# Hybrid S5 / RG-LRU / GLA block on one core: logarithms paced and moved, single PSUM banks in turn, head decays issued later, the FFN turn reordered

## The chip, the cores and the metric

One Trainium2 chip, one NeuronCore. The metric is device microseconds of one execution of the kernel; three runs are at hand.

## The reference, cut to what matters

One layer over 1024 latent tokens and 256 context tokens of width 1024: RMSNorm and modulation give `u` and `uc`; one projection `w_in` feeds three mixers; their outputs are gated, summed, projected and added; then a ConvFFN with a hidden width of 2816 follows. The places that the change touches compute

```python
zl = jnp.split(u @ w_in, cuts, axis=-1)          # ... also uc @ w_in
la = jax.nn.log_sigmoid(zd @ w2[d] + b2[d]) / GLA_TAU        # GLA's log decays, 16 ranks a direction
cum = jnp.cumsum(log_a, axis=3); k_out = k * jnp.exp(cum_last - cum)
y = jax.nn.gelu(y); y * jax.nn.sigmoid(y @ w_glu + b_glu)    # the S5 branch's GLU
hid = dwconv(u @ w_up, conv_w, conv_b, (1, 1))               # FFN, after the second norm
```

## The kernel before, in words

All large matmuls are done in a split form: an operand is held as a rounded high part and a rest, and three matmuls replace one (`mm3`, L283; `lat_steps`, L523; `v_steps`, L710). For a weight tile `split` (L213) makes the high part on ScalarE (`S.copy`, L214) and the rest on the engine named by `lo` (L215), which is GpSimd unless `wblock` (L221) is told otherwise. A weight tile is 128x1024; three buffers hold split tiles, two hold raw ones.

TensorE's order is the order of the text (`pe_order`, L444). The other engines are ordered ahead of time by a scheduler that places each instruction by its estimated time, with the text's order as priority, except in stretches whose order is written out (`norm_order`, L1770, and `turn_order`, L1932). Each engine then runs its list strictly in order. SP's list issues the loads and some stores.

The mixers' serial parts are small, so their TensorE pieces are set between pieces of one long projection stream. `proj_stream` (L743) is a generator; `F(name)` (L867) lets it run for the microseconds of the table `FILL` (L62). The stream's stages end in markers: "ctx", "lru" (context projections; then q, context k and v, and `z_steps`, L680), "pc" (latent k, `v_steps` over the eight latent blocks, "kv"; then g, "g"; the first gated products, "lru branch"; and the rest). `take` (L616) hands out the next split weight tile and `ahead` (L611) starts the following ones, so that up to two wait beyond the one in use.

Beside the stream runs `background` (L671), twelve steps of `decay_logs` (L649): four heads for each of two latent halves (128x512) and for the context (128x256). A step is one small product (two matmul records) into a PSUM bank `sm` (four of these), an Abs and a Relu on ScalarE that free the bank, an Exp, and a polynomial of three rounds, each a Square on ScalarE (L665) and a multiply-add on VectorE (L666) behind a first one (L662). GpSimd subtracts at the end (L667) and SP stores the result. After `z_steps` one step is started per `BG` = 4 us of stream.

In the order of time: the RG-LRU (L935 to L993), S5's prologue (L1014 to L1121, tables of powers, nearly all on VectorE), with `F("s5pro")` of 57.25 us at L1106 and `F("s5pro2")` of 12 us at L1251; eight S5 groups (3 us of stream as `s5st` and two times 1.5 us as `s5tr` in the first) (`s5_matrices`, `s5_states`, `s5_outputs`); the GLU (L1421 to L1460, 22 us of stream ahead of its products); four GLA heads (`Head`, L1278). A head's `decays` (L1284) are two scans (L1287, L1288), a difference (L1299) and an exponential (L1300); `keys` multiplies (L1307); TensorE transposes the result (L1331; `gtr`, 3.37 us of stream, stands ahead of head 0's). `states` ends in a chain of 18 multiply-adds (L1362). Then follow the merge, the output projection (L1709 to L1753, sixteen groups of 24 matmuls, `m` = 0 to 7 in two halves `j`), and the FFN's up-projection as a Strassen-Winograd product of `Pair`s (L1609). Between the two lies the turn (L1770 to L1891), with the second norm of the second half: `sums` and `bcast` on TensorE, `mul`, `sca`, `sub`, `hi`, `lo` on VectorE and ScalarE, and the first products `units(0)` to `units(3)`.

v_steps before takes two weight tiles for each half `hv` and runs two groups of four blocks through both:

```python
ws = take(2)
for b0 in range(0, len(blocks), 4):
    p = two()
    for i, b, k in [(i, b, 4 * kh + k) for kh in range(2) for i, b in enumerate(bs) for k in range(4)]:
```

Of the kernel before, what the change touches and what calls it, by code (L numbers as in the profile page):

```python
# [18 lines left out]
C = 256  # L19
# [18 lines left out]
def _parts(v, bits, n):  # L38
    out = []
    for _ in range(n):  # L40
# [41 lines left out]
        'gbc': [3.31, 3.0, 3.34, 3.52]}  # L82
BG = 4

# [25 lines left out]
def tile_kernel(tc, I, out, dbg=None):  # L110
# [30 lines left out]
    def mm():  # L141
        return psum[1].tile([128, 1024], F32, name=nm("mm"), tag="mm", bufs=psum[2])

    def two():

        return [one(t) for t in "ab"]

    def one(t="a"):
        return psum[1].tile([128, 512], F32, name=nm("m" + t), tag="m" + t, bufs=psum[2])
# [67 lines left out]
    def split_scaled(h, l, src, c):  # L217
        S.activation(h, src, AF.Copy, scale=c)
        V.scalar_tensor_tensor(l, src, c, f32(h), OP.mult, OP.subtract)

# [387 lines left out]

    wsrc, wq = [], [w0]

    def ahead(n):  # L611
        while len(wq) < n and wsrc:
            src = wsrc.pop(0)
            wq.append(wblock(src, src.shape[-1]))

# [33 lines left out]
    def decay_logs(o, n, z, w2):  # L649

        for h in range(4):
            p = sm()
            PE.matmul(p[:, :n], w2[:, h * 128:(h + 1) * 128], z[:, :n], start=True, stop=True)
            par = lsn[0] % 2
            lsn[0] += 1
            e = lsw[0][:, par * 512:par * 512 + n]
            acc = lsw[1][:, par * 512:par * 512 + n]
            S.activation(e, p[:, :n], AF.Abs, bias=vc("b2", h))
            r = tmp()[:, :n]
            S.activation(r, p[:, :n], AF.Relu, bias=nb2[:, h:h + 1], scale=-1.0)  # L660
            S.activation(e, e, AF.Exp, scale=-1.0)
            V.scalar_tensor_tensor(acc, e, LOGQ_R, e, OP.add, OP.mult)  # L662
            for i in range(3):
                q = tmp()[:, :n]
                S.activation(q, e, AF.Square, scale=LOGQ_S, bias=lqb[:, i:i + 1])  # L665
                V.scalar_tensor_tensor(acc, q, LOGQ_C[i], acc, OP.add, OP.mult)  # L666
            G.tensor_tensor(r, r, acc, OP.subtract)  # L667
            SY.dma_start(lsp[h][:, o:o + n], r)
            yield

    def background():  # L671
        zs, w2 = zw[0]
        for j in range(2):
            yield from decay_logs(C + j * 512, 512, zs[j], w2)
        yield from decay_logs(0, 256, zs[2], w2)
        reached.add("ls")

    zw = []

    def z_steps():  # L680
        wz = wraw(I["wz"], 256)
        zh, _ = whl()
        zz = zh[:, 0:512].rearrange("p (k m) -> p k m", k=KT)
        w2 = lsw[3][0:64, 256:768]
        SY.dma_start(w2, I["w2"])
        wz3 = wz.rearrange("p (k m) -> p k m", k=KT)
        S.copy(zz[:, :, 0:32], wz3)
        V.tensor_tensor(zz[:, :, 32:64], wz3, f32(zz[:, :, 0:32]), OP.subtract)
        p = one()
# [4 lines left out]
        zc = lsw[3][0:64, 0:256]  # L694
        S.copy(zc, p[0:64, 0:256])
        p = two()
        for k in range(KT):
            for j in range(2):
                PE.matmul(p[j][0:64], zz[:, k], uh[j][:, k], start=(k == 0), stop=False)
            for j in range(2):  # L700
                PE.matmul(p[j][0:64], zz[:, k], ul[j][:, k], start=False, stop=(k == KT - 1))
            yield 4 * COL
        zs = []
        for j in range(2):
            z = lsw[2][0:64, j * 512:(j + 1) * 512]
            S.copy(z, p[j][0:64])
            zs.append(z)
        zw.append((zs + [zc], w2))

    def v_steps(blocks):  # L710
        for hv in range(2):
            ws = take(2)
            for b0 in range(0, len(blocks), 4):
                bs = blocks[b0:b0 + 4]
                p = two()
                for i, b, k in [(i, b, 4 * kh + k) for kh in range(2) for i, b in enumerate(bs) for k in range(4)]:
                        o = p[i // 2][:, i % 2 * 256:(i % 2 + 1) * 256]
                        h, l = ws[k // 4]
                        sl = slice((k % 4) * 256, (k % 4 + 1) * 256)
                        if b < 2:  # L720
                            ah, al = uch[:, k, b * 128:(b + 1) * 128], ucl[:, k, b * 128:(b + 1) * 128]
                        else:
                            j, bb = divmod(b - 2, 4)
                            ah, al = uh[j][:, k, bb * 128:(bb + 1) * 128], ul[j][:, k, bb * 128:(bb + 1) * 128]
                        last = k == KT - 1 and i % 2 == 1
                        PE.matmul(o, ah, h[:, sl], start=(k == 0 and i % 2 == 0), stop=False, skip_group_check=True)
# [4 lines left out]
                for i0 in range(0, len(bs), 2):  # L731
                    t = pt()
                    S.copy(t, p[i0 // 2])
                    S.dma_start(vsp[bs[i0] * 128:(bs[i0] + 2) * 128, hv * 256:(hv + 1) * 256]
                                .rearrange("(a t) v -> t a v", a=2), t.rearrange("p (a v) -> p a v", a=2))

# [6 lines left out]
    def proj_stream():  # L743
# [12 lines left out]
        yield from both(xl1_out, lru_ctx)  # L756
        yield from marker("lru")
        for b in range(2):
            yield from lat(lambda p: out_rows(p, qsp[b]))
# [251 lines left out]
    def q5(tag=None):  # L1011
        return a5((128, 32), tag)

    lam = a5([128, 96])  # L1014
    SY.dma_start(lam, I["s5lam"])
# [234 lines left out]

    F("s5pro2")  # L1251
    cur = s5_matrices(0)
    for gb in range(8):
# [24 lines left out]
    class Head:  # L1278
# [59 lines left out]
        def states(self):  # L1338
# [22 lines left out]
            for step in range(1, 19):  # L1361
                V.scalar_tensor_tensor(Sd[:, step], Sd[:, step - 1], self.dec[:, step:step + 1], Sd[:, step],  # L1362
                                       OP.mult, OP.add)
            for c0 in (0, 8):
# [68 lines left out]
    for f in range(2):  # L1433
# [9 lines left out]
        V.scalar_tensor_tensor(y, z, 1.0, y, OP.add, OP.mult)  # L1443
        split_scaled(yh5[:, f], yl5[:, f], y, 2.0)
        YG.append(y)
# [20 lines left out]
    head = Head(0)  # L1466
    head.decays()
    head.keys()
# [10 lines left out]
    for h in range(4):  # L1479
# [5 lines left out]
        nxt = Head(h + 1) if h < 3 else None  # L1485
        head.scores(0)
        if nxt:
            nxt.decays()
        F("gsc")
# [119 lines left out]
    class Pair:  # L1609
# [101 lines left out]
    for j in range(2):  # L1711
        sl = tl[j]
        acc = pt()
        for m in range(8):
# [159 lines left out]
    q[0].z6()  # L1874
    q[0].load(3, 4)
    nxt.open("b")
    nxt.p6()
# [10 lines left out]
    q[1].load(3, 4)  # L1888
    q[1].z6()
    q[1].z57()  # L1890
    norm_order.__exit__(None, None, None)  # L1891
# [7 lines left out]
    for i in range(2, HID):  # L1899
# [11 lines left out]
        pair.load(2)  # L1911
        product(pair.D, pair.w[7], T3, True)
        pair.z57()
        pair.load(3, 4)
# [394 lines left out]
```

## Time and profile before

| | us |
|---|---|
| Runs | 1599.44, 1599.78, 1605.92 |
| Median | 1599.78 |
| The profiled execution, its own time | 1601.49 |
| Its span, first to last instruction | 1599.7 |
| TensorE busy in the span | 1521.8 |
| Mean granted TensorE clock | 0.983 of full speed |

The span and the 1.8 us around it make up the profiled execution's own time. Busy shares of a whole span mix stages with different limits, so the rows below are cut by stretches. "PEclk" is the granted share of TensorE's full clock: its two levels are 0.5 (1.2 GHz) and 1.0 (2.4 GHz), so a stretch at 0.95 ran a tenth of its time at the lower one.

### The profile page before, as it was taken

The numbers are of one execution on the slowest core, as the hardware profiler recorded it, in microseconds if no ns is written. First come the engines' busy times: TensorE is split into PE (matmuls) and PEld (weight loads), VectorE is DVE, ScalarE is ACT, GpSimd is POOL, SyncE is SP. The second block draws the span as 40 slices with busy tenths as digits, with TensorE's granted clock in tenths as the row PEclk, the third lists the DMA queues.
The fourth block names the chain that finished last, engine by engine and source line by source line (L and its number), as shares of the span: only waits on it lengthen the run. The fifth ranks groups of instructions, "written<-read, shape, count | busy, mean of one in ns | idle before, by whom it ended". The sixth has DMA issues, their size and how long they took to land. (4 is left out here: it accounts for less than half of the span.)

```text
span 1599.7 us, 21566 instructions
## 1 busy us (share of the span) xinstructions
PE 1521.8 (95%) x8144; PEld 1254.7 (78%) x8144; DVE 1092.8 (68%) x1620; ACT 770.1 (48%) x1221; POOL 461.3 (29%) x291
## 2 busy tenths in 40 slices
PE   5999999799998999999999988999999999999997
PEld 4888867677886788788888767788888888878887
DVE  4533469879876624533461689888888888899962
ACT  4423766665543643443233455444444444444661
POOL 3313333431122323222236534333333333000032
PEclk9999999899999999999999999999999999999999
DMA  9763633221224244231474321222222222974203
GB/s 346 242 224 93 208 109 110 93 90 58 64 61 144 70 139 130 77 86 60 144 246 159 130 88 40 92 80 79 80 91 81 80 80 100 370 248 157 93 27 106
DMA packets 93785, 198.91 MB, mean 124 GB/s; under 512 B 13489, under 2 KB 34865, under 8 KB 93553
## 3 DMA queue, kind: packets, MB, share of 16 engines
q1 hardware_dynamic: 81968, 181.62, 33.9%
q10 hardware_dynamic: 11712, 15.91, 2.9%
q8 instruction: 64, 1.05, 0.3%
q14 instruction: 41, 0.33, 0.1%
HBM read 158.98 MB, written 38.52 MB: 123 GB/s over the span
## 5 line engine op out<-in xcount | busy, mean ns | idle before, releaser
L215 POOL TENSOR_TENSOR wl<-wr,wh 128x1024 fp32r<-128x1024 f32 (+2 forms) x87 | 183.4, 2109 | 455.7 <-ACT wh L214 428.5
L214 ACT CAST wh<-wr 128x1024 fp32r<-128x1024 f32 (+2 forms) x87 | 77.3, 891 | 139.6 <-issue 41.9
L215 POOL TENSOR_TENSOR wp<-tmp,wp 128x512 fp32r<-128x512 f32 x44 | 74.1, 1701 | 220.4 <-ACT wp L214 203.4
L528 PE MATMUL ma<-uh,wh 128*128 128x512 f32 x272 | 118.0, 434 | 4.5 <-ACT pt L795 4.5
L528 PE MATMUL mb<-uh,wh 128*128 128x512 f32 x272 | 107.2, 394 | 0.0
L530 PE MATMUL ma<-ul,wh 128*128 128x512 f32 x272 | 107.0, 393 | 0.0
L530 PE MATMUL mb<-ul,wh 128*128 128x512 f32 x272 | 106.9, 393 | 0.0
L532 PE MATMUL mb<-uh,wl 128*128 128x512 f32 x272 | 106.7, 392 | 0.0
L532 PE MATMUL ma<-uh,wl 128*128 128x512 f32 x272 | 106.4, 391 | 0.0
L214 ACT CAST wp<-tmp 128x512 fp32r<-128x512 f32 x78 | 46.5, 619 | 93.0 <-DVE tmp L1629 92.9
L1693 DVE SCALAR_TENSOR_TENSOR ca<-gv,vec,ca 128x1023 f32<-128x1023 f32 (+2 forms) x66 | 61.4, 954 | 23.7 <-ACT ca L1685 23.6
L214 ACT CAST wp<-hd 128x512 fp32r<-128x512 f32 x88 | 52.8, 618 | 49.1 <-PE bkd L1998 25.9
L214 ACT CAST wp<-wr 128x512 fp32r<-128x512 f32 x97 | 58.2, 620 | 36.4 <-DMA wr<-in_wdn_dram 17.4
L1696 DVE SCALAR_TENSOR_TENSOR ca<-gv,vec,ca 128x1023 f32<-128x1023 f32 (+2 forms) x66 | 70.6, 1093 | 0.1
L528 PEld LDWEIGHTS ma<-uh,wh 128*128 128x128 f32 x272 | 51.8, 190 | 20.7 <-issue 6.5
L2178 POOL TENSOR_TENSOR acc<-acc,tmp 128x256 f32<-128x256 f32 (+1 forms) x9 | 9.0, 1002 | 182.8 <-ACT tmp L2175 182.7
L215 DVE TENSOR_TENSOR wp<-hd,wp 128x512 fp32r<-128x512 f32 x88 | 60.7, 708 | 1.3 <-ACT wp L214 1.1
L530 PEld LDWEIGHTS ma<-ul,wh 128*128 128x128 f32 x272 | 51.6, 190 | 11.5
L532 PEld LDWEIGHTS ma<-uh,wl 128*128 128x128 f32 x272 | 51.4, 189 | 11.5
L532 PEld LDWEIGHTS mb<-uh,wl 128*128 128x128 f32 x272 | 51.3, 189 | 11.4
L530 PEld LDWEIGHTS mb<-ul,wh 128*128 128x128 f32 x272 | 51.3, 189 | 11.3
L528 PEld LDWEIGHTS mb<-uh,wh 128*128 128x128 f32 x272 | 52.0, 191 | 9.5 <-issue 1.4
(628 smaller groups left out, 4661.9 us busy)
## 6 DMA issues: line engine op xcount, KB each, us to landing
wa<-in_ada_dram SPq DMA_DIRECT2D x96, 256.0 KB
wr<-in_wup_dram SPq DMA_DIRECT2D x46, 512.0 KB
wr<-in_win_dram SPq DMA_DIRECT2D x40, 512.0 KB
wr<-in_wdn_dram SPq DMA_DIRECT2D x22, 512.0 KB
hd<-hid SPq DMA_DIRECT2D x22, 512.0 KB
hid<-ca SPq DMA_DIRECT2D x21, 512.0 KB
wr<-in_wout_dram SPq DMA_DIRECT2D x16, 512.0 KB
tmp<-in_wdn_dram SPq DMA_DIRECT2D x22, 256.0 KB
```

Source lines behind the costliest of these rows:

```text
L214: S.copy(h, src)
L215: lo.tensor_tensor(l, src, f32(h), OP.subtract)
L528: PE.matmul(p[j], h[:, kk], uh[j][:, k], start=f, stop=False)
L530: PE.matmul(p[j], h[:, kk], ul[j][:, k], start=False, stop=False)
L532: PE.matmul(p[j], l[:, kk], uh[j][:, k], start=False, stop=e)
L1693: V.scalar_tensor_tensor(a[:, t0_ + 1:t0_ + 1 + n1], x[:, o:o + n1], fw[0], a[:, t0_ + 1:t0_ + 1 + n1], OP.mult, OP.add)
L1696: V.scalar_tensor_tensor(a[:, t0_ + c - 1:t0_ + n - 1], x[:, o + c:o + n], fw[2], a[:, t0_ + c - 1:t0_ + n - 1], OP.mult, OP.add)
L2178: G.tensor_tensor(acc, acc, sq, OP.add)
```

## The change

- `BG` goes from 4 to 6: a step of the logarithms per 6 us of stream. The context's steps come first.
- In `decay_logs` the Relu's output moves from a `tmp` buffer to `lsw[3]`, and the last subtraction goes from GpSimd to VectorE. The second latent half of z lies in partitions 64 to 127, with a second copy of `w2` there (one more load).
- `z_prep` loads and splits the weights of z at the start of the stream's stage after "lru"; they lie in a `tmp` buffer and no longer in a split-weight buffer.
- `one()` takes PSUM banks of the kinds a and b in turn. `v_steps` opens a bank for every two blocks at once, takes one weight tile at a time, runs all blocks through it, and copies each bank out as its last matmul is issued.
- `rests[0]`: between L1014 and L1254 the rests of the stream's weight tiles are made by VectorE.
- Head 0's decays are ordered on VectorE behind the last split of the GLU's input, and the next head's behind the last multiply-add of this head's states (`tc.issue_after` orders the block's instructions on the given instruction's own engine behind it).
- In the output projection four subtractions go from GpSimd at `m` = 1 to VectorE at `m` = 3 (second half). In the turn q[1].p1 stands before `sums`, one product before `bcast`, and z57's copy of bank C is a step of its own, `c57`, set before `hi(5, 2)` and, for q[1], where it was.

The diff, cut:

```diff
-BG = 4
+BG = 6
...
-    def one(t="a"):
+    def one(t=None):
+
+        if t is None:
+            ones_[0] += 1
+            t = "ab"[ones_[0] % 2]
...
-            wq.append(wblock(src, src.shape[-1]))
+            wq.append(wblock(src, src.shape[-1], rests[0]))
...
-            r = tmp()[:, :n]
+            r = lsw[3][:, par * 512:par * 512 + n]
...
-            G.tensor_tensor(r, r, acc, OP.subtract)
+            V.tensor_tensor(r, r, acc, OP.subtract)
...
-        zs, w2 = zw[0]
+        zs, zc, w2 = zw[0]
+        yield from decay_logs(0, 256, zc, w2[0])
         for j in range(2):
-            yield from decay_logs(C + j * 512, 512, zs[j], w2)
-        yield from decay_logs(0, 256, zs[2], w2)
+            yield from decay_logs(C + j * 512, 512, zs[j], w2[j])
...
-    def z_steps():
+    def z_prep():
+
+
         wz = wraw(I["wz"], 256)
-        zh, _ = whl()
-        zz = zh[:, 0:512].rearrange("p (k m) -> p k m", k=KT)
-        w2 = lsw[3][0:64, 256:768]
-        SY.dma_start(w2, I["w2"])
+        zz = tmp([128, 512], F32R).rearrange("p (k m) -> p k m", k=KT)
+        w2 = [lsw[2][64 * j:64 * j + 64, 512:1024] for j in range(2)]
+        for w in w2:
+            SY.dma_start(w, I["w2"])
...
         for hv in range(2):
-            ws = take(2)
-            for b0 in range(0, len(blocks), 4):
...
+            p = [one("ab"[(i + hv) % 2]) for i in range(len(blocks) // 2)]
+            for kh in range(2):
+                (h, l), = take()
+                for i, b in enumerate(blocks):
+                    o = p[i // 2][:, i % 2 * 256:(i % 2 + 1) * 256]
+                    for k in range(4):
...
+                    if kh and i % 2:
+                        t = pt()
+                        S.copy(t, p[i // 2])
...
     def v_steps(blocks):
...
         for hv in range(2):
-            ws = take(2)
-            for b0 in range(0, len(blocks), 4):
...
+            p = [one("ab"[(i + hv) % 2]) for i in range(len(blocks) // 2)]
+            for kh in range(2):
+                (h, l), = take()
+                for i, b in enumerate(blocks):
+                    o = p[i // 2][:, i % 2 * 256:(i % 2 + 1) * 256]
...
+                    if kh and i % 2:
+                        t = pt()
+                        S.copy(t, p[i // 2])
...
         yield from marker("lru")
+        z_prep()
...
+    rests[0] = V
     lam = a5([128, 96])
...
     F("s5pro2")
+    rests[0] = G
...
-        split_scaled(yh5[:, f], yl5[:, f], y, 2.0)
+        glu_last = split_scaled(yh5[:, f], yl5[:, f], y, 2.0)
...
-    head.decays()
+    with tc.issue_after(glu_last.ins):
+        head.decays()
...
         if nxt:
-            nxt.decays()
+            with tc.issue_after(head.last.ins):
+                nxt.decays()
...
+        def c57(self):
+            S.copy(self.gv[1][:, tl[0]], self.C)
+
         def z57(self):
             w, z = self.gv[1][:, tl[0]], self.gv[1][:, tl[1]]
-            S.copy(w, self.C)
...
             if j == 1 and m == 3:
+                for k in range(4, KT):
+                    x = hT[k][:, tl[0]]
+                    V.tensor_tensor(x, x, hT[k - 4][:, tl[0]], OP.subtract)
...
-                    if k > 3:
-                        x = hT[k][:, tl[0]]
-                        G.tensor_tensor(x, x, hT[k - 4][:, tl[0]], OP.subtract)
...
+    q[1].p1()
     q[1].sums((5,))
...
-    q[1].p1()
     rq = rstd_cols(st, 4, small[:, 12:16])
+    product(q[0].A, q[0].w[2], B21, False)
...
     bcast(pr, rq, 4)
+    product(q[1].A, q[1].w[2], B21, False)
     for i in range(2):
-        product(q[i].A, q[i].w[2], B21, False)
...
     q[0].load(3, 4)
+    q[0].c57()
...
     q[1].z6()
+    q[1].c57()
     q[1].z57()
```

## Rows read from the trace of the kernel before

**Rows 1.** The page's part on busy time, TensorE's line

```profile
PE 1521.8 (95%) x8144; PEld 1254.7 (78%) x8144; DVE 1092.8 (68%) x1620; ACT 770.1 (48%) x1221; POOL 461.3 (29%) x291
```

**Rows 2.** Busy time by stretch: stretch, length, engines with instruction counts, PEclk, DMA

```profile
200.00:226.00 26.00, 22.12 (x163) 15.44 (x162) 17.43 (x16) 20.34 (x24) 11.02 (x4) 0.93 0.40 128
255.00:336.00 81.00, 67.19 (x445) 60.22 (x446) 71.20 (x171) 54.58 (x93) 34.17 (x18) 0.92 0.28 94
336.00:402.00 66.00, 61.14 (x311) 50.30 (x310) 56.36 (x111) 39.17 (x67) 12.44 (x8) 0.95 0.23 71
490.00:526.00 36.00, 31.35 (x129) 24.64 (x128) 27.70 (x23) 21.52 (x30) 11.58 (x6) 0.91 0.51 145
640.00:672.00 32.00, 28.24 (x163) 22.76 (x162) 20.45 (x30) 14.46 (x25) 7.67 (x5) 0.95 0.22 80
895.00:985.00 90.00, 77.93 (x321) 60.30 (x321) 76.50 (x92) 47.67 (x78) 44.18 (x27) 0.96 0.24 81
```

**Rows 3.** What TensorE waited for, whole span: us in total, times, longest

```profile
PE ma L726 <- ACT wh L214: 7.6, 1, 7.6
...
PE bkc L839 <- ACT gv L1666: 4.6, 1, 4.6
PE ma L528 <- ACT pt L795: 4.5, 2, 3.8
PE ma L691 <- DVE wh L688: 3.9, 1, 3.9
PE sm L653 <- ACT tmp L660: 3.7, 2, 2.8
...
PE sm L285 <- DVE s L219: 2.9, 1, 2.9
PE sm L286 <- POOL wl L215: 2.5, 1, 2.5
PE ma L727 <- POOL wl L215: 2.4, 1, 2.4
...
PE bkb L279 <- DVE pt L1730: 1.6, 1, 1.6
```

**Rows 4.** GpSimd's groups by shape, 217 to 337 us: busy, mean ns, idle before

```profile
L215 POOL TENSOR_TENSOR wl<-wr,wh 128x1024 fp32r<-128x1024 f32 x9 | 24.5, 2727 | 20.1 <-ACT wh L214 20.1
L667 POOL TENSOR_TENSOR tmp<-tmp,lsw 128x512 f32<-128x512 f32 x8 | 14.3, 1793 | 32.4 <-DVE lsw L666 28.6 <-issue 3.8
```

**Rows 5.** VectorE's costliest group by shape, 217 to 337 us

```profile
L666 DVE SCALAR_TENSOR_TENSOR lsw<-tmp,lsw 128x512 f32<-128x512 f32 x24 | 16.4, 683 | 0.2
```

**Rows 6.** Timeline of one VectorE and one GpSimd instruction: start, us, instruction

```profile
303.80 2.54 DVE L662 SCALAR_TENSOR_TENSOR lsw<-lsw 128x256 f32<-128x256 f32 x1 [1.16 <-POOL tmp L667]
...
303.72 2.34 POOL L215 TENSOR_TENSOR wl<-wr,wh 128x1024 fp32r<-128x1024 f32 x1
```

**Rows 7.** Timeline: the first S5 transposes' last operand, and the transposes

```profile
316.53 0.41 DVE L1162 TENSOR_TENSOR s<-s,s 128x256 f32<-128x256 f32 x1
...
335.29 0.38 PE L1166 MATMUL sm<-con,s 128*128 128x128 f32 x2
```

**Rows 8.** VectorE's timeline around the GLU, and TensorE's at head 0's transposes

```profile
501.63 2.82 DVE L1287 TENSOR_TENSOR_SCAN gl<-gl,gl 64x1280 f32<-64x1280 uint8 x1 [1.51 <-DMA gl<-lsp]
...
521.47 1.49 DVE L1307 TENSOR_TENSOR gl<-gl,gl 128x1280 f32<-128x1280 f32 x1 [0.30 <-ACT gl L1300]
...
524.45 1.25 PE L1331 MATMUL sm<-con,gl 128*128 128x128 f32 x10
```

**Rows 9.** ScalarE's timeline in head 1

```profile
662.97 1.27 ACT L1300 ACTIVATE gl<-gl 128x1280 f32<-128x1280 f32 x1 [4.79 <-DVE gl L1299]
```

**Rows 10.** GpSimd's groups, 895 to 985 us

```profile
L1752 POOL TENSOR_TENSOR h<-h,h 128x512 f32<-128x512 f32 x4 | 6.0, 1509 | 8.5 <-DVE B21l L215 8.5
```

**Rows 11.** Timeline at the end of the turn: VectorE, then TensorE

```profile
975.19 0.67 DVE L1667 TENSOR_TENSOR gv<-gv,bkd 128x512 f32<-128x512 f32 x1
...
979.09 0.39 PE L839 MATMUL bkd<-T4h,wp 128*128 128x512 f32 x1
```

More of the change, by code (lines that the diff above doesn't have):

```diff
@@ L142, in mm @@
         return psum[1].tile([128, 1024], F32, name=nm("mm"), tag="mm", bufs=psum[2])
+    ones_ = [0]
     def two():
         return [one(t) for t in "ab"]
-    def one(t="a"):
+    def one(t=None):
+        if t is None:
+            ones_[0] += 1
+            t = "ab"[ones_[0] % 2]
         return psum[1].tile([128, 512], F32, name=nm("m" + t), tag="m" + t, bufs=psum[2])
@@ L218, in split_scaled @@
         S.activation(h, src, AF.Copy, scale=c)
-        V.scalar_tensor_tensor(l, src, c, f32(h), OP.mult, OP.subtract)
+        return V.scalar_tensor_tensor(l, src, c, f32(h), OP.mult, OP.subtract)
     def wblock(src, cols=1024, lo=G):
@@ L607, in gate_out @@
             S.dma_start(tsp[m][:, j * 512:(j + 1) * 512], t)
-    wsrc, wq = [], [w0]
+    wsrc, wq, rests = [], [w0], [G]
     def ahead(n):
@@ L671, in background @@
     def background():
-        zs, w2 = zw[0]
+        zs, zc, w2 = zw[0]
+        yield from decay_logs(0, 256, zc, w2[0])
         for j in range(2):
-            yield from decay_logs(C + j * 512, 512, zs[j], w2)
-        yield from decay_logs(0, 256, zs[2], w2)
+            yield from decay_logs(C + j * 512, 512, zs[j], w2[j])
         reached.add("ls")
-    zw = []
-    def z_steps():
+    zw, zp = [], []
+    def z_prep():
         wz = wraw(I["wz"], 256)
-        zh, _ = whl()
-        zz = zh[:, 0:512].rearrange("p (k m) -> p k m", k=KT)
-        w2 = lsw[3][0:64, 256:768]
-        SY.dma_start(w2, I["w2"])
+        zz = tmp([128, 512], F32R).rearrange("p (k m) -> p k m", k=KT)
+        w2 = [lsw[2][64 * j:64 * j + 64, 512:1024] for j in range(2)]
+        for w in w2:
+            SY.dma_start(w, I["w2"])
         wz3 = wz.rearrange("p (k m) -> p k m", k=KT)
@@ L688, in z_steps @@
         V.tensor_tensor(zz[:, :, 32:64], wz3, f32(zz[:, :, 0:32]), OP.subtract)
+        zp.append((zz, w2))
+    def z_steps():
+        zz, w2 = zp[0]
         p = one()
@@ L693, in z_steps @@
             yield COL
-        zc = lsw[3][0:64, 0:256]
-        S.copy(zc, p[0:64, 0:256])
+        zct = tmp([64, 256])
+        S.copy(zct, p[0:64, 0:256])
         p = two()
@@ L704, in z_steps @@
         for j in range(2):
-            z = lsw[2][0:64, j * 512:(j + 1) * 512]
+            z = lsw[2][64 * j:64 * j + 64, 0:512]
             S.copy(z, p[j][0:64])
             zs.append(z)
-        zw.append((zs + [zc], w2))
+        zw.append((zs, zct, w2))
     def v_steps(blocks):
         for hv in range(2):
-            ws = take(2)
-            for b0 in range(0, len(blocks), 4):
[L714 to L719, printed above, removed]
+            p = [one("ab"[(i + hv) % 2]) for i in range(len(blocks) // 2)]
[4 more added lines that the diff above has]
+                    for k in range(4):
+                        sl = slice(k * 256, (k + 1) * 256)
+                        ka = 4 * kh + k
                         if b < 2:
-                            ah, al = uch[:, k, b * 128:(b + 1) * 128], ucl[:, k, b * 128:(b + 1) * 128]
+                            ah, al = uch[:, ka, b * 128:(b + 1) * 128], ucl[:, ka, b * 128:(b + 1) * 128]
                         else:
                             j, bb = divmod(b - 2, 4)
-                            ah, al = uh[j][:, k, bb * 128:(bb + 1) * 128], ul[j][:, k, bb * 128:(bb + 1) * 128]
-                        last = k == KT - 1 and i % 2 == 1
-                        PE.matmul(o, ah, h[:, sl], start=(k == 0 and i % 2 == 0), stop=False, skip_group_check=True)
+                            ah, al = uh[j][:, ka, bb * 128:(bb + 1) * 128], ul[j][:, ka, bb * 128:(bb + 1) * 128]
+                        last = ka == KT - 1 and i % 2 == 1
+                        PE.matmul(o, ah, h[:, sl], start=(ka == 0 and i % 2 == 0), stop=False, skip_group_check=True)
                         PE.matmul(o, ah, l[:, sl], start=False, stop=False, skip_group_check=True)
@@ L730, in v_steps @@
                             yield 3 * COL
[L731 to L735, printed above, removed]
+                    if kh and i % 2:
+                        t = pt()
+                        S.copy(t, p[i // 2])
+                        S.dma_start(vsp[(b - 1) * 128:(b + 1) * 128, hv * 256:(hv + 1) * 256]
+                                    .rearrange("(a t) v -> t a v", a=2), t.rearrange("p (a v) -> p a v", a=2))
     def marker(name):
@@ L1361, in states @@
             for step in range(1, 19):
-                V.scalar_tensor_tensor(Sd[:, step], Sd[:, step - 1], self.dec[:, step:step + 1], Sd[:, step],
-                                       OP.mult, OP.add)
+                self.last = V.scalar_tensor_tensor(Sd[:, step], Sd[:, step - 1], self.dec[:, step:step + 1],
+                                                   Sd[:, step], OP.mult, OP.add)
             for c0 in (0, 8):
@@ L1912, in tile_kernel @@
         product(pair.D, pair.w[7], T3, True)
+        pair.c57()
         pair.z57()
```

## The prediction
> **What bounds the kernel now.** I read the page's busy times first: TensorE works 1521.8 us of the span [rows 1], so the kernel is bound by TensorE and the change, which leaves its matmuls as they are, can only take away waits and time at the lower clock. All other engines have room on average, but averages mix stages. So I then read the waits of TensorE [rows 3]: few, long and single, each at another place, and each with a releaser on another engine. Then I cut the span into stretches around those waits [rows 2]. The loss of a stretch has two parts: its length less TensorE's busy time, and the share that the clock lacks. PEclk of 0.93 over 26 us means that 0.07 x 26 = 1.8 us were lost to the lower level (1.2 GHz), partly while TensorE stood still, where it costs nothing. Every stretch with a long wait has such a loss, so a wait that goes takes its low clock with it.
>
> The sum is made against the profiled execution's own time, 1601.5 us; the median of the runs is 1.7 us below that, and I take the 1.7 off at the end. About 8 us, 0.5%, is what a measurement of this kernel tells from no change.
>
> **z_prep.** TensorE waits 3.9 us in L691 for z's split weights (VectorE L688) [rows 3]. The change loads and splits them a whole stage earlier, so the wait has nothing left to wait for; the load, the cast and the split run beside the q projections. The stretch loses 26 - 22.1 = 3.9 us and 1.8 us of clock [rows 2], 5.7 at most; since a part of the clock's loss lies in the wait itself, I take **-5.0**. Three loads go ahead of the stage's weight loads on SP's list; they are small, and two split tiles stand ready beyond the one in use, which covers them. If the buffer in `tmp` held up another user, the gain would be zero.
>
> **The logarithms and v_steps.** From 255 to 336 us TensorE is idle 81 - 67.2 = 13.8 us, of which the three waits in L653, L726 and L727 make 3.7, 7.6 and 2.4 [rows 2, 3]; the clock lacks 0.08 x 81 = 6.5 us, of which I count half, 3.3, because the longest wait lies in it. L653 waits for a free bank `sm`: steps are started faster than Abs and Relu come round behind the ping-pong of Square and multiply-add. One step per 6 us of stream in place of 4 takes that wait away, all 3.7. L726 waits for ScalarE's cast of a weight tile. The old v_steps holds both split tiles through all its blocks, so no buffer is free for the next cast until the end of a half; the new one gives a tile back after 96 matmuls, and the next cast starts a whole tile earlier. I count its 7.6 as gone, and keep the 2.4 of L727, the rest, as a doubt, since the rest now stands in VectorE's strict order. 3.7 + 7.6 + 3.3 = 14.6, so **-14.6** (bounds 0 and 20.3, which is 13.8 + 6.5).
>
> **VectorE in S5's prologue, the cover of all this.** VectorE is busy 71.2 of the same 81 us [rows 2]. The change adds nine rests [rows 4]; a 128x512 multiply-add takes 0.683 us [rows 5], so a 128x1024 rest is some 1.37, together 12.3. It adds twelve subtractions: eight of 0.68 and four half as wide of 0.41 [rows 5, 7], 7.1. That is 19.4 us more. Three things are taken off. First, the rests (24.5 us) and the subtractions (14.3 us) leave GpSimd [rows 4], and beside GpSimd VectorE's instructions with two operands stand still: L662 on 128x256 took 2.54 us while a rest of 2.34 us ran [rows 6], where an instruction of that size takes 0.41 [rows 7]. That is 2.1 us lost beside one GpSimd instruction; there are seventeen in rows 4, so between 0 and 17 x 2.1 = 36 us come back. I take half, 18. Second, twelve steps took 48 us of stream and now take 72, and `s5pro` is 57.25: some two and a half steps of 4 x 0.683 + 0.683 = 3.4 us go behind the prologue, 8 us. Together 71.2 + 19.4 - 18 - 8 = 64.6 us in the 81 - 14 = 67 that remain. It fits, just.
>
> The reader should see what is late next: the first S5 transposes (L1166). Their last operand was ready at 316.9 and they ran at 335.3, 18.4 us of slack [rows 7]. TensorE will now come 5.0 + 14.6 = 19.6 us earlier, and the slack is used up to within an instruction or two; the groups that follow ask for VectorE every few us. I add a new wait of **+4**, between 0 (VectorE moves up as it is relieved) and +12 (only half of the 18 come back and a low clock follows).
>
> The Trainium skill, in "Perfetto Trace Analysis", section "Optimizing Scalar/DVE Operations", says that GpSimd and VectorE share a read port of SBUF, so that moving work between the two might not help. By that the 18 us would be nothing and the new wait 12 or more; by the rows the same subtraction costs 1.79 us on one engine and 0.68 on the other [rows 4, 5], so I keep +4.
>
> **The GLU.** L284 and L285 wait for the split of its input, the longest 2.9 us [rows 3]; the stretch is idle 36 - 31.35 = 4.65 and lacks 0.09 x 36 = 3.2 of clock [rows 2]. Head 0's two scans of 2.82 us stand among that work [rows 8]. Moved behind it they free 5.6 us, more than the stall. But the same VectorE work then lies between the GLU and head 0's transposes. VectorE has only 1.5 + 0.3 us of idle between the scan and L1307 [rows 8], so L1307, which ended at 522.96, ends at 521.2 at best, and TensorE, which came to the transposes at 524.45 [rows 8], gains at most 3.3 there; `gtr` covers the rest. With some low clock behind a second wait I take **-2** (bounds -7.9 and +1).
>
> **Head 1's decays.** L528 waits up to 3.8 us for a copy out of PSUM (L795) [rows 3] that stands on ScalarE behind the exponential L1300 of the next head, which itself waits 4.8 us for VectorE [rows 9]. Ordered behind the chain of 18, the block has this head's scores, outputs and norm as its cover. The stretch is idle 3.76 and lacks 1.6 of clock [rows 2], 5.4 at most: **-4.5**. `issue_after` orders VectorE only; that ScalarE follows is the data's doing, since L1300 cannot be placed ahead of its operand.
>
> **The four subtractions.** L286 waits 2.5 us for a rest on GpSimd [rows 3] that stands behind four subtractions of 1.5 us each [rows 10]. On VectorE at `m` = 3 they cost 4 x 0.68 = 2.7 us [rows 5] beside the output projection. The stretch lacks 0.04 x 90 = 3.6 us of clock [rows 2] around two waits, 1.8 each: 4.3 at most, **-4.0** (bounds -4.3 and +2.7, if VectorE is the later engine there).
>
> **The turn.** L839 waits 4.6 us for the copy of bank C (L1666), and `sums` 1.6 for VectorE's L1730 [rows 3]. With p1 ahead of it the latter is covered. With `c57` early the third product can start at once, but the fourth needs bank D, read by L1667 until 975.9; it started at 979.1 [rows 11]. So no more than 3.2 us come of it, and `bcast` is now one product later, which moves the VectorE chain behind it by about 1. I take **-2** (bounds -8.0, which is 4.6 + 1.6 + 1.8, and +1.5).
>
> **Single banks in turn** cost nothing that I can see. v_steps holds four banks at once, all there are of kinds a and b, but between a bank's last matmul and the first of its next use lie those of two pairs of blocks at least, 48 of them, and the copy of a bank is one instruction of ScalarE. Without that distance each half would end in a wait for a copy, as L528's in [rows 3].
>
> Sum: -5.0 - 14.6 + 4 - 2 - 4.5 - 4.0 - 2 = -28.1; 1601.5 - 28.1 - 1.7 = 1571.7 us.
>
> **Rivals.** First, everything goes: no new wait, GLU and turn with their whole losses: 5.7 + 17.9 + 7.9 + 5.4 + 4.3 + 8.0 = 49 (17.9 is 14.6 and half of what it leaves), 1551 us. For it speaks that each wait has its own cause; against it the unbroken VectorE queue in both places. Second, VectorE is not relieved: the prologue takes 12 us more than I count, 1584 us. For it: VectorE is busy in 71.2 of 81 us as it is. The Trainium skill's rule above would end here too. Third, the change does not do what it says: ScalarE still stands in its old order at the casts and in head 1, and only z's weights, L653, the subtractions and the turn come: 5.0 + 3.7 + 4.0 + 2 = 14.7, 1585 us. For it: the scheduler places by estimates, and ScalarE has no written order there. Fourth, slower: VectorE's strict order holds a rest behind S5's tables, and TensorE waits for each of the nine tiles. GpSimd made nine in 120 us, one in 13 [rows 4], and two may be ready ahead, so this decides once a rest comes 27 us behind its cast. The price is a wait like L727's, 2.4, and a low clock of 1.8 each: 9 x 4.2 = 38 us, against 5.0 + 2 + 4.5 + 4.0 + 2 = 17.5 gained: 1601.5 + 20.5 - 1.7 = 1620 us. Against it: VectorE's rest is half as long as GpSimd's, and VectorE always has idle time within 27 us.
>
> **The numbers.** Forecast 0.53 (1562 to 1582); everything 0.10; VectorE not relieved 0.18, a third of it so far that it lies within 8 us of before; orders unchanged 0.11, half of it within 8 us; slower 0.08. Faster 0.53 + 0.10 + 0.12 + 0.05 = 0.80, same 0.06 + 0.06 = 0.12, slower 0.08. The range runs from 1553, most of the way to the second case, to 1592, past the third and fourth.
>
> **What would show it.** Right: no wait in L691, L653 or L726; a wait of a few us with a VectorE releaser in the first S5 groups; L1331 or what stands behind it waiting for L1307; the turn's wait on bkd in place of bkc. Wrong: waits for `wl` with VectorE as releaser between 230 and 330 us; L1166 waiting over 10 us; L795 still behind L1300; GpSimd gone and VectorE's L662 still at 2.5 us.

## The result and the profile after

The changed kernel takes 1577.53 us (median of 4 runs, 1576.69 to 1578.69); the kernel before took 1602.55 in the same comparison (1599.44 to 1605.92). The ratio is 0.9844, 95% interval 0.9817 to 0.9871: 25 us faster. 1571.7 was forecast, with 1553 to 1592 around it.

The sum came out within 6 us, but not by its terms. The page of the profiled execution first, TensorE's line, to be held against [rows 1]:

```profile
PE 1513.6 (96%) x8144; PEld 1248.9 (79%) x8144; DVE 1096.1 (70%) x1645; ACT 772.3 (49%) x1223; POOL 414.6 (26%) x266
```

The same matmuls, 8 us less of busy time (a part of the low clock that went), and GpSimd 47 us less. Next the waits of TensorE, to be held against [rows 3]; the first and third lie in the first 30 us, where nothing was changed:

```profile
PE sm L285 <- DVE sp L912: 12.7, 1, 12.7
PE sm L1347 <- DVE gl L1323: 12.6, 1, 12.6
PE ma L434 <- ACT uh L323: 4.9, 1, 4.9
PE mb L711 <- ACT pt L746: 4.8, 1, 4.8
PE bkd L853 <- DVE gv L1688: 4.0, 2, 3.1
```

Of the waits of [rows 3] only 1.1 us of the GLU's (L285, now L291) and 0.7 of the copies' (L528, now L534) are left, and the turn's wait of 4.6 at bank C (L839) has become 4.0 at bank D (L853). Two new ones stand there: 12.6 us in L1347 (L1331 before: head 0's transposes) for the keys' multiply L1323 (L1307), and 4.8 us in L711 (z's latent product) for a copy of v_steps. The stretches, to be held against [rows 2]; their bounds follow the work, so they lie elsewhere on the clock:

```profile
202.60:230.30 27.70, 22.92 (x164) 15.75 (x163) 19.77 (x19) 22.46 (x25) 2.39 (x1) 0.88 0.39 134
230.30:321.00 90.70, 90.70 (x552) 76.25 (x551) 82.26 (x199) 63.95 (x104) 5.27 (x3) 1.00 0.33 106
321.00:381.00 60.00, 58.69 (x312) 47.61 (x311) 58.27 (x117) 45.48 (x76) 12.14 (x6) 1.00 0.25 75
465.00:514.00 49.00, 35.17 (x156) 28.89 (x157) 33.60 (x25) 23.87 (x34) 19.36 (x10) 0.86 0.42 121
621.00:653.00 32.00, 32.00 (x190) 26.05 (x189) 15.83 (x28) 16.04 (x26) 8.26 (x6) 1.00 0.25 83
871.00:961.00 90.00, 82.89 (x344) 65.28 (x343) 82.89 (x102) 51.56 (x85) 40.91 (x24) 0.94 0.24 82
```

In the second, S5's prologue, TensorE has no idle time at all and the full clock. In the fourth it is idle 13.8 us and lacks 14% of the clock: the GLU and head 0's transposes are now the worst stretch of the kernel.

Where the time came from is read at landmarks: the start of the same matmul in both traces. The difference between two landmarks is what the stretch between them gave.

| TensorE's landmark (line before) | before | after | difference | the stretch gave | forecast |
|---|---|---|---|---|---|
| modulation, 641st of L310 | 194.8 | 197.4 | +2.6 | +2.6 | 0 |
| end of the RG-LRU's gates, L957 | 226.3 | 230.3 | +4.0 | **+1.4** | -5.0 |
| first S5 transposes, L1166 | 335.3 | 320.3 | -15.0 | **-18.9** | -14.6 |
| last S5 outputs, L1245 | 487.4 | 466.6 | -20.8 | **-5.9** | +4 |
| head 0's transposes, L1331 | 524.5 | 509.7 | -14.7 | **+6.1** | -2 |
| head 2's transposes, L1331 | 637.3 | 622.3 | -15.0 | -0.3 | 0 |
| last head's outputs, L1393 | 751.2 | 732.2 | -19.1 | **-4.1** | -4.5 |
| first up-projection, L839 | 927.1 | 903.7 | -23.4 | **-4.3** | -4.0 |
| end of the turn, 61st of L839 | 984.6 | 960.7 | -23.9 | **-0.5** | -2 |
| last matmul but a few, L273 | 1591.8 | 1568.4 | -23.3 | +0.6 | 0 |

The first row is taken for chance: TensorE's first wait was 11.6 us in the trace before and 12.7 in this one, and lies between 11.7 and 13.0 in the other traces below; by 34 us, where every trace is at the same matmul and they differ by up to 2.9 us, 2.2 of the 2.6 are there. Terms of both signs are off by 4 to 10 us and nearly cancel.

### The profile page after: what moved, and what is told of

The parts are those of the page before. It is cut to its first block, busy times and chain, and to the rows that moved or that the text cites. A ratio compares the mean times of both kernels' runs of the same rounds, so it can differ in the third digit from the quotient of the medians.

```text
span 1576.6 us, 21571 instructions
## 1 busy us (share of the span) xinstructions
PE 1513.6 (96%) x8144; PEld 1248.9 (79%) x8144; DVE 1096.1 (70%) x1645; ACT 772.3 (49%) x1223; POOL 414.6 (26%) x266
## 5 line engine op out<-in xcount | busy, mean ns | idle before, releaser
L221 POOL TENSOR_TENSOR wl<-wr,wh 128x1024 fp32r<-128x1024 f32 (+1 forms) x78 | 164.2, 2105 | 477.1 <-ACT wh L220 432.8
L534 PE MATMUL ma<-uh,wh 128*128 128x512 f32 x272 | 116.9, 430 | 0.7 <-ACT pt L809 0.7
L534 PE MATMUL mb<-uh,wh 128*128 128x512 f32 x272 | 106.7, 392 | 0.0
L1378 DVE SCALAR_TENSOR_TENSOR gl<-gl,gl 128x128 f32<-128x128 f32 x72 | 31.2, 433 | 53.1 <-ACT gl L1376 35.6
L534 PEld LDWEIGHTS ma<-uh,wh 128*128 128x128 f32 x272 | 51.3, 189 | 15.4 <-issue 5.2
L534 PEld LDWEIGHTS mb<-uh,wh 128*128 128x128 f32 x272 | 51.4, 189 | 9.6 <-issue 1.4
```

Of the source, the lines that this page charges most:

```text
L221: lo.tensor_tensor(l, src, f32(h), OP.subtract)
L534: PE.matmul(p[j], h[:, kk], uh[j][:, k], start=f, stop=False)
L1378: self.last = V.scalar_tensor_tensor(Sd[:, step], Sd[:, step - 1], self.dec[:, step:step + 1], Sd[:, step], OP.mult, OP.add)
```

## The experiments

Times are medians. Twelve kernels: eight take one part out of the changed kernel or mend one place of it (1577.5 us), three put one part alone into the kernel before, one puts two gains together.

**1. Head 0's order undone.**

```diff
-    with tc.issue_after(glu_last.ins):
-        head.decays()
+    head.decays()
```

> The changed kernel with head 0's decays no longer ordered behind the GLU's last split. Theory (the order moved the wait and made it longer): the GLU's products wait again, 4 to 5 us and a low clock of 3, and the wait of 12.65 us at head 0's transposes goes, since the VectorE chain from the GLU's first multiply to the keys is 25.5 us long without the order and 33.2 with it. 4 to 7 us faster than the changed kernel, about 1572 us. Rival (the same VectorE work lies ahead of the transposes in either order, as predicted): within 2 us of the changed kernel, 1576 to 1580.

Measured: 1569.33 us (ratio to before 0.9793, 0.9773 to 0.9812), 8.2 us **faster than with the order**. The theory holds, its size a little exceeded. The wait for the keys is gone and the GLU's are back:

```profile
PE sm L290 <- ACT s L224: 3.7, 1, 3.7
PE sm L291 <- DVE s L225: 2.6, 1, 2.6
```

VectorE's timeline says why. In the changed kernel, from the GLU's first multiply to the keys (start, duration):

```profile
476.45 0.69 DVE L1455 TENSOR_SCALAR s<-s 128x1024 f32<-128x1024 f32 x1 [2.87 <-ACT s L1454]
...
493.09 4.79 DVE L1304 TENSOR_TENSOR_SCAN gl<-gl,gl 64x1280 f32<-64x1280 uint8 x1
...
500.18 3.65 DVE L1315 TENSOR_TENSOR gl<-gl,gl 128x1280 f32<-128x1280 f32 x1
503.76 1.07 DVE L1474 SCALAR_TENSOR_TENSOR s<-tmp,s 128x512 f32<-128x512 f32 x1
...
507.56 2.12 DVE L1323 TENSOR_TENSOR gl<-gl,gl 128x1280 f32<-128x1280 f32 x1 [2.73 <-ACT gl L1316]
```

and in experiment 1:

```profile
474.40 0.69 DVE L1455 TENSOR_SCALAR s<-s 128x1024 f32<-128x1024 f32 x1 [2.76 <-ACT s L1454]
...
485.96 2.82 DVE L1304 TENSOR_TENSOR_SCAN gl<-gl,gl 64x1280 f32<-64x1280 uint8 x1
...
495.41 1.49 DVE L1315 TENSOR_TENSOR gl<-gl,gl 128x1280 f32<-128x1280 f32 x1
...
499.84 1.52 DVE L1323 TENSOR_TENSOR gl<-gl,gl 128x1280 f32<-128x1280 f32 x1
```

From the first multiply to the end of the keys it is 509.7 - 476.45 = 33.2 us with the order and 501.4 - 474.4 = 27.0 without. The scan takes 4.79 us in place of 2.82, the difference 3.65 in place of 1.49, the keys 2.12 in place of 1.52: 4.7 us together, each beside one of these instructions of GpSimd in the changed kernel.

```profile
492.00 3.20 POOL L221 TENSOR_TENSOR wl<-wr,wh 128x1024 fp32r<-128x1024 f32 x1 [4.98 <-ACT wh L220]
500.15 2.34 POOL L221 TENSOR_TENSOR yb<-s,yb 128x1024 fp32r<-128x1024 f32 x1 [4.95 <-ACT yb L220]
505.98 2.36 POOL L221 TENSOR_TENSOR yb<-s,yb 128x1024 fp32r<-128x1024 f32 x1 [3.50 <-ACT yb L220]
```

Another 2.4 us pass between the end of the difference, 503.8, and the exponential's start (L1316, 506.3), against 1.4 in experiment 1; the exponential stands on ScalarE behind a cast of the GLU's output that waits for L1474. Moved behind the GLU, the block met work that it had not met before. TensorE, 6.5 us quicker through the GLU, came to the transposes at 497.1 and stood until 509.7.

**2. More stream ahead of head 0's transposes.**

```diff
-        'gtr': [3.37, 4.7, 3.88, 4.43],
+        'gtr': [16.0, 4.7, 3.88, 4.43],
```

> The changed kernel with 16.0 us of stream ahead of head 0's transposes in place of 3.37, taken from the stream that is left after the heads. Theory (TensorE waits 12.65 us there for keys that only VectorE's chain makes, and nothing later takes it back): the wait falls below 1 us, the low clock around it goes, 12 to 15 us faster than the changed kernel, about 1563.5 us. Rival (VectorE's chain then ends later too, or the stream that is missed after the heads leaves waits there): at most 6 us faster, 1571 us or more.

Measured: 1563.99 us (0.9761, 0.9741 to 0.9782), 13.5 us faster than the changed kernel. Theory: the wait is gone, and the stream, of which 36 us were left behind the last head's outputs and 22 still are, is not missed later. So the wait cost its full length and nothing behind it took it back.

**3. z's context product in a bank of kind a.**

```diff
         zz, w2 = zp[0]
-        p = one()
+        ones_[0] += 1
+        p = one("a")
```

> The changed kernel with the context's product of z in a bank of kind a; the count of turns goes on as before. Theory (the wait of 4.78 us at z's latent product is for the second bank of kind b, which v_steps' copy frees late because ScalarE stands in the RG-LRU's activations): no wait there, no low clock behind it, 5 to 7 us faster than the changed kernel, about 1571.5 us. Rival (ScalarE is late whatever the bank): the wait moves to the next product that needs a bank, and the time stays within 2 us of 1577.5.

Measured: 1575.10 us (0.9825, 0.9807 to 0.9842), 2.4 us faster: between the two. The wait in L711 and its low clock are gone, but the wait for ScalarE returns in part in the modulation's matmuls, which want a bank `sm` that ScalarE empties in L973:

```profile
PE sm L316 <- ACT lt L973: 4.1, 2, 2.8
```

ScalarE's timeline in the changed kernel shows the queue. The context's v_steps end at 208 us; the copy of their second bank (L746, `mb`) runs at 215.1, behind activations of the RG-LRU, two casts and a load of the activation table:

```profile
208.48 1.26 ACT L982 ACTIVATE lw<-la 128x1280 f32<-128x1280 f32 x1
...
210.21 1.99 ACT L220 CAST wh<-wr 128x1024 fp32r<-128x1024 f32 x2
...
212.59 1.28 ACT L984 ACT_TABLE_LOAD   x1
213.89 1.27 ACT L984 ACTIVATE lw<-lw 128x1280 f32<-128x1280 f32 x1
215.06 0.57 ACT L746 COPY pt<-mb 128x512 f32<-128x512 f32 x1
```

z's context product had taken the other bank of kind b by its turn, and the latent product needed this one. Between the landmarks at 195 and 226 us this kernel gives -2.8 where the changed one gives +1.4. Of these 4.2 us 1.5 are lost again by head 0's transposes, where TensorE waits for the keys in either kernel.

**4. The next heads' order undone.**

```diff
-            with tc.issue_after(head.last.ins):
-                nxt.decays()
+            nxt.decays()
```

> The changed kernel with the next heads' decays no longer ordered behind the last multiply-add of the states; head 0's order stays. Theory (that order alone took away the wait of 3.76 us for the copy out of PSUM in head 1, with its low clock): the wait is back and the time is 4 to 5.5 us longer, about 1582 us. Rival (the wait went because VectorE and ScalarE meet head 1 at other times now): within 1.5 us of 1577.5.

Measured: 1583.70 us (0.9881, 0.9863 to 0.9898), 6.2 us slower: the theory, its size exceeded. The wait for L795's copy (L809) is back to the tenth, and 1.5 us more in head 0's outputs:

```profile
PE ma L534 <- ACT pt L809: 4.5, 2, 3.8
```

The wait lies between head 2's transposes and head 3's (622.4 and 685.1 us here, 62.7 apart against 58.3 in the changed kernel; 637.3 and 699.6 before). It is therefore head 2's, not head 1's, as the prediction, [rows 9] and the expectation call it.

**5. The rests of the prologue back on GpSimd.**

```diff
-    rests[0] = V
+    rests[0] = G
```

> The changed kernel with the nine rests of S5's prologue back on GpSimd. In the changed kernel the first S5 transposes' last operand is ready 17 us before TensorE comes. Theory (VectorE's relief is real but TensorE does not need it: v_steps' early release of tiles and the slower steps took the waits away): VectorE's multiply-adds show blocked instructions of 2 us and more again, the operand comes up to 9 us later, inside the slack, and the time stays within 2.5 us of 1577.5. Rival (the prologue needs the rests on VectorE): waits for the rests or in the first S5 groups, 6 us or more slower, 1583.5 or above.

Measured: 1586.21 us (0.9895, 0.9879 to 0.9912), 8.7 us slower: the rival. The expectation's 17 us are the slack of the earlier of two operands; the later one has 10.7 us in the changed kernel and 11.8 here. Of the loss 2 us lie ahead of the first S5 transposes and 6 in the S5 groups, where TensorE now waits for VectorE and ScalarE:

```profile
PE mb L534 <- DVE pt L606: 1.6, 1, 1.6
PE sm L1202 <- DVE s L1236: 1.4, 1, 1.4
```

The rests themselves, from 217 to 330 us (busy, mean ns):

```profile
L221 POOL TENSOR_TENSOR wl<-wr,wh 128x1024 fp32r<-128x1024 f32 x7 | 26.7, 3817 | 64.5 <-ACT wh L220 64.5
```

The mean of 3.8 us is one rest's doing: six took 2.4 to 2.9 us, about as in [rows 4], and the seventh 11.6.

```profile
302.77 11.62 POOL L221 TENSOR_TENSOR wl<-wr,wh 128x1024 fp32r<-128x1024 f32 x1 [12.53 <-ACT wh L220]
```

VectorE ran twenty instructions without a pause beside it, so VectorE seems to hold GpSimd as GpSimd holds VectorE. In the changed kernel VectorE makes a rest in 1.2 us, with one of 2.2 (201 to 321 us):

```profile
L221 DVE TENSOR_TENSOR wl<-wr,wh 128x1024 fp32r<-128x1024 f32 x9 | 11.9, 1333 | 1.6 <-ACT wh L220 1.5
```

**6. The pace back to 4 us.**

```diff
-BG = 6
+BG = 4
```

> The changed kernel with a step of the logarithms per 4 us of stream again. Theory (the pace took away the waits in the step's product for a free bank, 3.7 us with low clock, and moved some 10 us of VectorE's work behind the prologue): the waits for ScalarE at the step's product are back, 3 to 6 us slower, about 1582 us. Rival (the cheaper subtraction alone makes a step fit into 4 us): within 2 us of 1577.5.

Measured: 1581.84 us (0.9868, 0.9848 to 0.9889), 4.3 us slower. The size is the theory's and the place is not: no wait at the steps' product, but one of 3.4 us for v_steps' copy on ScalarE, with low clock.

```profile
PE mb L739 <- ACT pt L746: 3.4, 1, 3.4
```

**7. The steps' subtraction back on GpSimd.**

```diff
-            V.tensor_tensor(r, r, acc, OP.subtract)
+            G.tensor_tensor(r, r, acc, OP.subtract)
```

> The changed kernel with the last subtraction of a step back on GpSimd, twelve of them. Theory (it frees VectorE of some 7 us and blocks it for more, all inside 17 us of slack): within 2 us of 1577.5. Rival (the steps' interval becomes longer than their pace): waits for a bank at the step's product, 4 us or more slower.

Measured: 1584.13 us (0.9875, 0.9853 to 0.9896), 6.6 us slower: the rival's size, again by v_steps' copy (2.5 us and a low clock behind it), not by a wait at the steps' product.

```profile
PE ma L534 <- ACT pt L746: 2.5, 1, 2.5
```

**8. The earlier v_steps in the changed kernel** (the function of the kernel before, word for word).

> The changed kernel with the earlier v_steps: two weight tiles held through two groups of four blocks. Theory (its late release of the tiles made the wait of 7.6 us for a cast, the 2.4 us for a rest and the low clock between): these come back, 9 to 13 us slower, about 1588.5 us. Rival (ScalarE's queue behind the ping-pong of the steps made that wait, and the pace cured it): within 3 us of 1577.5.

Measured: 1573.40 us (0.9816, 0.9800 to 0.9832), 4.1 us **faster**. The theory falls. No wait for a cast comes back, and z's wait for a bank goes, as in experiment 3. From the end of the gates to the first S5 transposes both forms give the same 18.9 us. Beside the other parts the new v_steps is worth nothing there and costs 4 us at z.

What, then, took away the 7.6 us of L726? Three parts alone, each put into the kernel before.

**9. The pace alone** (`BG` = 6 and nothing else).

> The kernel before with nothing but the slower pace, a step of the logarithms per 6 us of stream. Theory (the wait of 7.6 us for a weight tile's cast came from ScalarE's queue, in which the cast stood behind squares of steps that came too fast): the waits for the cast, for the rest and for a bank of the steps go, 12 to 17 us faster than before, about 1587 us. Rival (it came from GpSimd's blocking of VectorE, on which the squares wait): only the steps' own wait of 3.7 us goes, 3 to 6 us faster, about 1597 us.

Measured: 1600.37 us against 1604.12 (0.9975, 0.9964 to 0.9987), 3.7 us: the rival's size. The steps' own wait is gone, and so is the 7.6 us in L726, but the late engines show elsewhere:

```profile
PE ma L727 <- POOL wl L215: 4.8, 1, 4.8
...
PE mb L528 <- ACT pt L733: 3.4, 1, 3.4
```

By the landmarks the stretch from the gates to the first S5 transposes gives 7.8 us, and the S5 groups lose 4.2 of it again (156.3 us against 152.2).

**10. Rests and subtractions on VectorE alone.**

```diff
-            wq.append(wblock(src, src.shape[-1]))
+            wq.append(wblock(src, src.shape[-1], rests[0]))
...
-            G.tensor_tensor(r, r, acc, OP.subtract)
+            V.tensor_tensor(r, r, acc, OP.subtract)
...
+    rests[0] = V
...
+    rests[0] = G
```

> The kernel before with nothing but the nine rests and the twelve subtractions moved from GpSimd to VectorE. Theory (GpSimd's instructions held VectorE, VectorE held ScalarE's squares, these held the cast): the waits for the cast and the rest go, the steps' wait falls under 1 us, and the first S5 groups lose their waits of 2.0 and 2.5 us: 14 to 22 us faster than before, about 1584 us. Rival (the pace is what counts, or VectorE, given 19 us more, becomes the late engine): at most 5 us faster.

Measured: 1587.74 us (0.9898, 0.9880 to 0.9916), 16.4 us: the theory. The cast's and the rest's waits are gone; the steps' stays at 2.2 us, more than expected, and of S5's two waits one stays. Two thirds of the whole gain is this one move.

```profile
PE sm L1246 <- DVE s L1231: 3.8, 3, 2.5
...
PE sm L653 <- ACT tmp L660: 2.9, 2, 2.2
```

**11. The new v_steps alone.**

> The kernel before with nothing but the new v_steps. Theory as predicted (the tiles' early release lets the cast start a tile earlier): the waits of 7.6 and 2.4 us and their low clock go, 8 to 12 us faster than before, about 1592 us, though z's products may wait for a bank. Rival (the release was never what held the cast, since with the other parts in place the earlier v_steps shows no such wait): ScalarE is as late as before, at most 3 us faster, and a wait for v_steps' copy of a bank stands in its place.

Measured: 1596.89 us (0.9954, 0.9938 to 0.9970), 7.2 us: nearer the predicted size, but not by the predicted way. The wait for the cast is exchanged for a longer one for a copy of a bank, and TensorE comes to the first S5 transposes 0.5 us later than before; the 7 us are gained in the S5 groups and the GLU behind them. Why there was not tried; VectorE has the later operand of those transposes ready at 308.7 us, against 316.9 in [rows 7].

```profile
PE mb L727 <- ACT pt L734: 10.6, 1, 10.6
```

ScalarE's timeline of this kernel shows who holds it (start, duration, in brackets the idle time and its releaser):

```profile
286.50 0.57 ACT L734 COPY pt<-ma 128x512 f32<-128x512 f32 x1
292.00 0.72 ACT L665 ACTIVATE tmp<-lsw,small 128x512 f32<-128x512 f32 x1 [4.93 <-DVE lsw L666]
...
296.38 0.56 ACT L734 COPY pt<-mb 128x512 f32<-128x512 f32 x1
```

A square waits 4.9 us for VectorE's multiply-add, and the copy stands behind it. VectorE's timeline shows that the multiply-add (L666) was not slow itself; it stood behind table steps of S5 that were:

```profile
287.77 2.31 DVE L1112 TENSOR_SCALAR s<-s 128x32 f32<-128x32 f32 x1
290.00 0.17 DVE L1114 TENSOR_SCALAR s<-s 128x32 f32<-128x32 f32 x1
290.09 1.28 DVE L1161 TENSOR_TENSOR s<-s,s 128x256 f32<-128x256 f32 x1
291.29 0.68 DVE L666 SCALAR_TENSOR_TENSOR lsw<-tmp,lsw 128x512 f32<-128x512 f32 x1
```

L1112 took 2.31 us where the next one of its shape took 0.17, beside a rest on GpSimd:

```profile
287.26 2.79 POOL L215 TENSOR_TENSOR wl<-wr,wh 128x1024 fp32r<-128x1024 f32 x1
```

Cast or copy, whatever is next on ScalarE is late. So each of the three parts alone takes the 7.6 us of L726 away by name; the pace and v_steps put other waits in its place, and only experiment 10 does not.

**12. Two gains together:** the earlier v_steps and 16 us of stream at head 0.

> The changed kernel with the earlier v_steps and 16.0 us of stream ahead of head 0's transposes. Theory (the two gains of 4.1 and 13.5 us lie at different places and add): no wait for z's bank, none over 1 us at head 0's transposes, 1577.5 - 17.6 = 1560 us, 1558 to 1562. Rival (TensorE comes earlier to head 0, so that 16 us of stream no longer cover VectorE's chain): 1562 us or more, with a wait for the keys.

Measured: 1561.03 us (1559.69 to 1562.94; ratio to before 0.9730, 0.9712 to 0.9748): the theory. It beats both kernels, the changed one by 16.5 us. Its longest waits behind the first 30 us:

```profile
PE sm L316 <- ACT lt L971: 4.4, 2, 3.0
PE bkd L852 <- DVE gv L1687: 4.0, 2, 3.1
```

## Why the prediction was right, point by point

**The total** was right by luck: errors of both signs met. By the landmarks the sum was -28.1 and the traces show -23.3, of which +2.6 is the chance of the start.

**z_prep, and single banks in turn.** The wait in L691 went as said. The step that failed is "single banks in turn cost nothing that I can see": it looked at v_steps' own four banks in the latent half, not at the products that come after the context's. There only the 16 of z's context product lie between, and the copy came 7 us after its bank's last matmul; a distance of 48, some 6 us, would not have been enough either. -5.0 became +1.4; with the bank of the other kind -2.8, and the remainder went to the modulation's wait for ScalarE.

**The logarithms and v_steps.** -14.6 was forecast and -18.9 came, from another cause. "The old v_steps holds both split tiles, so no buffer is free for the next cast" is not what decides: in experiment 8 the old v_steps shows no such wait, and in experiment 11 the new one has its cast in time, at 284.4 us in place of 302.0, and TensorE stands still all the same. The cause is a chain: GpSimd's instructions held VectorE's [rows 6], and the multiply-adds stood behind what was held (the 24 on 128x512 of [rows 5] took 0.683 us on average and 0.689 in experiment 10, so few were held themselves); the multiply-adds held ScalarE's squares, and the squares held the casts and copies in ScalarE's strict order. That the move of the work decides is shown by experiment 10, 16.4 us from the move alone; the links are read from the traces. Experiment 10 does not tell the rests from the subtractions, nor the shorter rests (1.2 us for 2.4 and more) from the end of the holding; put back one at a time, they cost 8.7 and 6.6 us (experiments 5 and 7). The pace, to which I gave the 3.7 us of L653, is worth 3.7 us in all by itself (experiment 9) and 4.3 among the others.

**VectorE's cover.** The +4 failed in sign. The first S5 operands were the thing to look at, but they moved too. [rows 7] has the later of the two, which in the changed kernel is the second line here:

```profile
302.90 0.45 DVE L1177 TENSOR_TENSOR s<-s,s 128x256 f32<-128x256 f32 x1
...
309.16 0.46 DVE L1177 TENSOR_TENSOR s<-s,s 128x256 f32<-128x256 f32 x1
...
320.33 0.38 PE L1181 MATMUL sm<-con,s 128*128 128x128 f32 x2
```

Ready at 309.6, before transposes at 320.3, it has 10.7 us of slack against the 18.4 of [rows 7]: TensorE came 15.0 us earlier and the operand 7.3. The step that failed is the one from VectorE's 64.6 us to the slack. By that sum VectorE was relieved of 6.6 us, yet all of TensorE's gain was charged to an operand that stayed at 316.9. I had also left out that the S5 groups, whose waits of 2.0 and 2.5 us were VectorE's, would gain. The relief itself, 18 us, was well sized: between the gates and the first S5 transposes VectorE's instructions beside GpSimd took 22.7 us more than the shortest of the same line and shape in any of these traces, and 3.8 in the changed kernel, so 18.9 came back (an estimate from the traces' durations). -5.9 came where +4 was forecast, and experiment 5 shows waits of the forecast kind in the S5 groups when only the rests are put back.

**The rule on GpSimd and VectorE.** The Trainium skill's sentence, that moving work between the two might not help ("Perfetto Trace Analysis", section "Optimizing Scalar/DVE Operations"), is not borne out here: the move alone is worth 16.4 us. What does fit is the Trainium skill's "SBUF — State Buffer", section "Who interferes with whom": an instruction of VectorE with two inputs in SBUF and one of GpSimd that reads SBUF lock each other out. The traces agree (2.54 us in [rows 6] for 0.41 in [rows 7], 4.79 for 2.82 above). L1112 in experiment 11, held as well, has one tensor input. That the work is cheaper when one engine has all of it fits this, but no run separates the lock from the shorter rest.

**The GLU and head 0.** The mechanism was named (the keys become late for the transposes), and the size was wrong beyond its bounds: "ends at 521.2 at best", that is 24 us behind the GLU's first multiply at 497.4 of the trace before, was taken as what it would be. It became 33.2, by GpSimd's blocking and by ScalarE's order, and TensorE came 6.5 us sooner. +6.1 in place of -2. This one term is 8 us, more than the miss of the total. Order without its cover was a loss; with the cover (experiment 2) it is the better of the two, 1564.0 against 1569.3 (more stream without the order was not tried).

**Head 1's decays (head 2's by the traces), the four subtractions, the turn.** -4.1 against -4.5, and -4.3 against -4.0: both as worked out, the first shown by experiment 4. The turn's wait moved from bank C to bank D, as said:

```profile
952.66 0.67 DVE L1688 TENSOR_TENSOR gv<-gv,bkd 128x512 f32<-128x512 f32 x1
...
953.48 0.47 PE L853 MATMUL bkd<-T4h,wp 128*128 128x512 f32 x1 [3.15 <-DVE gv L1688]
```

VectorE's L1688 came 22.5 us earlier than L1667 in [rows 11], while TensorE was 23.4 us ahead at the start of the FFN: its chain was set back by 0.9 us, near the 1 that was taken for the moved `bcast`. The stretch gave 0.5 us in place of 2. The subtractions and the turn were not tried by themselves; their sizes are the landmarks'.

**The rivals.** No rest came so late that TensorE waited for it in the prologue, so the slower one did not come; nor did the second, since TensorE has no idle time in S5's prologue, nor the third, since both orders took.

## What to carry to other kernels

A wait names the engine that came last, not the one that is to blame: the 7.6 us "for a cast" go back in the main, by way of two engines, to GpSimd, and only parts put in one at a time could tell. Look at the single instructions behind a mean, too: one rest of 11.6 us made six ordinary ones look slow. An order that takes a block out of one wait needs its length in independent work ahead of its own consumer; move the filler together with the order. A buffer taken in turn is only as free as the slowest engine that empties it, so follow the turn into the next stage.

## What the runs showed of the hardware that was not expected

GpSimd and VectorE cost each other time in both directions: VectorE's scan lost 2.0 us to a single rest on GpSimd, and a rest on GpSimd, mostly 2.4 to 2.9 us, took 11.6 beside an unbroken run of VectorE in experiment 5; on VectorE itself it took 1.2. And TensorE's first wait differs by more than a microsecond between runs (11.6 to 13.0 us), a part of each difference between single traces that no edit explains.
